# Small experts and extra slots as whole float32 matmuls on column tiles of the array, with unsplit weights

## Chip, cores and metric

The kernel runs on one core of a Trainium2 chip. Its time is the device time of one execution in microseconds. The engines are named as in the profile: PE (TensorE matmul), PEld (its weight loads), DVE (VectorE), ACT (ScalarE), POOL (GpSimd) and SP (SyncE, which here issues the weight transfers).

## What is computed

The reference is two layers of a decoder trunk over 256 tokens of width 1024. In each layer three token mixers (S5, SSD, gated DeltaNet) are followed by a feed-forward part: a dense SwiGLU in the first layer, and in the second eight SwiGLU experts of which each token uses two. The change lies in the second layer's experts alone:

```python
def moe_ffn(h, w_router, w_gate, w_up, w_down):
    logits = (h @ w_router).astype(jnp.float32)
    top_v, top_i = lax.top_k(logits, TOP_K)
    ...
    for e in range(N_EXPERTS):
        out = out + combine[..., e:e + 1].astype(h.dtype) * swiglu(h, w_gate[e], w_up[e], w_down[e])
    return out
```

`swiglu(h)` is `(silu(h @ w_gate) * (h @ w_up)) @ w_down`, with gate and up of 1024 x 3584 and down of 3584 x 1024, all float32. Eight experts have 352 MB of weights, which pass through the chip once.

## The kernel before

**Slots.** An expert works only on the tokens that chose it. `route` ranks the tokens of each expert, and a one-hot matrix gathers them into slots (`take_in`, tile `xe`) and later puts the results back (`put_back`). Experts 0, 1 and 7 have 128 slots ("wide"), the others 64 ("small"), and expert 7 has 16 more ("few", the extra slots). If an expert has more tokens than its slots, a general path (`general`, `expert`) runs in place of `stream`; the inputs here take `stream`.

**Precision.** Every weight is split into a high part in float32r (`his`, a copy on ACT) and a low part (`los`, a subtraction on DVE); `stage` does that for a load of 128 x 2048 values. A wide product is three float32r matmuls, in `mm3`: high by high, high by low, low by high. A small expert has its 64 tokens' high and low parts side by side in 128 columns of the array, so two matmuls (with `his` and with `los`) make all four products (`half_up`, `half_down`). Its accumulator has 128 rows then, high and low, and they are summed as they are transposed, by a matmul with a matrix of ones (`turn_sum`, tile `pmts`). The extra slots are done alike, in 32 columns (`pmf`, `pfd`), with their down products added up in the SBUF (`accf`).

**Steps.** An expert's 3584 hidden columns are done in 7 steps of 512. A step has the gate and up products (`pmg`), the gate (`sg`, or `gf` and `sgs`), its transposition (`pmt` of a wide expert, `pmts` of a small one), and the down products (`macc`), which come one step later. It uses 6 loads of 1 MiB: two of gate, two of up, two of down. `STEPS` orders the steps: expert 2 alone, expert 0 alone, then seven rounds of one step of expert 7 with three steps of experts 3, 4 and 5, then expert 1 alone and expert 6 alone. The gather of a coming expert is cut into pieces that stand between a step's products (`GATHER`, `gap`).

**Transfers.** The loads go through a ring of ten slots of 1 MiB (`ringb` 0 to 4, then `ringa` 0 to 4), all issued by SP in the order of use. A load waits until what last read its slot is done: in before that is `stage`. Before the routing four loads are staged ahead (two with GpSimd as the subtracting engine, into `extra`), and the first step's gate and up products stand ahead of the branch between `stream` and `general`.

**Order.** A scheduler orders the instructions of each engine when the program is built, with its own estimate of times; engines then run their queues in order.

Of the kernel before, what the change touches and what calls it, by code (L numbers as in the profile page):

```python
# [27 lines left out]
# schedule: engines of the first layer's S5 weights, offsets of priority of the mixers' parts (by layer), pieces of the last  # L28
# weights, engines of the first staged weights, the order around the FFN, and the steps of it beside the second S5 weights
# [5 lines left out]
TP = [2, 2, 4, 2, 0, 1]  # L35
MO = [[0, 1, 1, 1], 1]
# [9 lines left out]
def tile_hymba_trunk(ctx: ExitStack, tc: tile.TileContext, p: dict, out: bass.AP):  # L46
# [43 lines left out]
    # ------------------------------------------------------------------ constants  # L90
# [67 lines left out]
    # columns: norm_mix 0, norm_ffn 16, ssd conv 32, its bias 88, ssd_norm 102, s5_norm 108, gdn_norm 112  # L158
# [21 lines left out]
    # ------------------------------------------------------------------ helpers  # L180
# [23 lines left out]
    def stage(src, after=None, parts=1, on=V):  # L204
        k, n = src.shape[1], src.shape[2]
        pool, words = cur['stg']
        if isinstance(pool, list):
            his, los = pool
            h, l = (q[cur['sn'] % len(q)][:, :k * n].rearrange("p (k n) -> p k n", k=k) for q in (his, los))
            cur['sn'] += 1  # L210
            for o in pieces(k, n, parts):
                if after is None:
                    A.activation(out=h[o], in_=src[o], func=AF.Copy)  # L213
                else:
                    A.activation(out=h[o], in_=src[o], func=AF.Identity, scale=after)
                on.tensor_tensor(out=l[o], in0=src[o], in1=h[o].bitcast(F32), op=OP.subtract)  # L216
            return h, l
        h = pool.tile([128, words], F32R, name="whi", tag="whi")[:, :k * n].rearrange("p (k n) -> p k n", k=k)
        l = pool.tile([128, words], F32R, name="wlo", tag="wlo")[:, :k * n].rearrange("p (k n) -> p k n", k=k)
        cur['last', 'A'] = A.activation(out=h, in_=src, func=AF.Copy)  # L220
        cur['last', 'V'] = on.tensor_tensor(out=l, in0=src, in1=h.bitcast(F32), op=OP.subtract)  # L221
        return h, l
# [18 lines left out]
    def exact_exp(o, x, t, q):  # L241
        """o = exp(x) to float32 accuracy; t, q: scratch like x."""
# [24 lines left out]
    def rows_rstd(pool=None):  # L267
        """of X: the rows' mean squares (with the norm's guard) and their reciprocal roots"""
# [10 lines left out]
    def along(r, pool):  # L279
        """a column [128, 2] of the tokens as a row in each partition"""  # L280
# [7 lines left out]
    def rows_T(wcol, pool, scaled=False):  # L288
        """X, scaled by the norm's weight, transposed and split; the rows' scale is put on after the products"""
# [22 lines left out]
    # ------------------------------------------------------------------ S5 weights  # L312
# [8 lines left out]
    # powers of the discretised poles, for both layers: [state, layer * tile]  # L321
# [8 lines left out]
    def s5_small():  # L330
# [55 lines left out]
        # unit phases exp(i theta 2^k), k = 2..7, brought back to modulus 1 on the way  # L386
# [24 lines left out]
    def s5_prep(l, keep, ET, EB, EC, tag="S"):  # L411
        """in three steps"""
# [11 lines left out]
        # rotation tables over 64 positions, step exp(4 i theta)  # L424
# [12 lines left out]
        # input matrices [state, tile, 4 positions of a block, 32 channels]  # L437
# [28 lines left out]
        # output matrices  # L466
# [25 lines left out]
        # lag matrices, with the skip weight on the diagonal  # L492
# [21 lines left out]
    # ------------------------------------------------------------------ mixers  # L514
# [63 lines left out]
    def layer_mix(l, pm):  # L578
# [26 lines left out]
        # ---- GDN projections  # L605
# [11 lines left out]
        # gates  # L617
# [3 lines left out]
        for n in range(2):  # L621
# [6 lines left out]
            # without the rows' scale  # L628
# [14 lines left out]
        # softplus = max(x,0) + log1p(exp(-|x|)), log1p(e) = 2 atanh(e/(2+e))  # L643
# [37 lines left out]
        # sums of squares of q, k per token and head  # L681
# [23 lines left out]
        # (in the second layer the S5 scratch lies beside its weights, and is free with them before the rest is)  # L705
# [3 lines left out]
        with scope("late", "right"):  # L709
# [21 lines left out]
            # ---- GDN token-layout operands  # L731
# [24 lines left out]
            # ---- GDN pair matrices  # L756
# [66 lines left out]
            # ---- GDN recurrence over the two chunks  # L823
# [17 lines left out]
            def gdn_out(n):  # L841
                # norm per head, gate
# [7 lines left out]
                # of 64 times the mean; the eight that its root lacks is in the norm's weight  # L850
# [51 lines left out]
            # ---- S5  # L902
# [10 lines left out]
            with using(pm):  # L913
                mark('ssdp', l)
                # ---- SSD
# [56 lines left out]
                    # states shifted by one position, rotated back  # L972
# [19 lines left out]
                    # 2*gelu  # L992
                    # beyond |y| = 12 the tanh is 1 in float32
# [29 lines left out]
                    # squares of 2^-10 y, limited so that their sum stays finite; a mean square that  # L1023
                    # float32 cannot hold has a zero reciprocal root
# [29 lines left out]
            with scope("ssd"):  # L1054
# [62 lines left out]
                # the gates are without the rows' scale: the guard is over its square  # L1117
# [26 lines left out]
        # ---- output projection  # L1144
# [84 lines left out]
    # ------------------------------------------------------------------ MoE  # L1229
    def route(split_rows, cw, rk, cnt, one, r):  # L1230
        caps = act.tile([1, 8], F32, name="caps")
        G.memset(caps, 64.0)
        for e in range(NE):
            if SLOTS[e] != 64:
                G.memset(caps[:, e:e + 1], SLOTS[e] + 16.0 * (e == MANY))
# [18 lines left out]
        with ExitStack() as st:  # L1254
            if MO[1]:
# [4 lines left out]
        # the two largest, the first of equal ones first  # L1260
# [13 lines left out]
        # exclusive count of equal ones before, plus the number above  # L1274
# [3 lines left out]
        # (of these the inclusive count is at most two)  # L1278
# [3 lines left out]
        # rank of a token among the tokens of an expert, from one on; zero where it isn't one  # L1282
# [6 lines left out]
        def rest():  # L1289
# [7 lines left out]
            V.tensor_scalar(out=one, in0=rk[:, 0, 0:1], scalar1=0.0, scalar2=1.0, op0=OP.mult, op1=OP.add)  # L1297
            # the weights of the two, with the rows' scale of what the experts return
# [4 lines left out]
            # (the table of the gates is loaded here)  # L1303
# [9 lines left out]
    # the stream of experts: their slots, those interleaved, those gathered together, and the one with sixteen slots more  # L1313
    SLOTS = {0: 128, 1: 128, 2: 64, 3: 64, 4: 64, 5: 64, 6: 64, 7: 128}
    # (of the expert with more, a step to each three of the small ones beside it)
# [7 lines left out]
    PLACE = {(2, 0): (256, 64), (0, 0): (0, 128), (7, 0): (256, 128), (7, 128): (512, 16), (3, 0): (0, 64), (4, 0): (128, 64),  # L1323
# [502 lines left out]
```

## Time and profile before

| | |
|---|---|
| median of 3 runs | 1725.63 us (1724.66 to 1727.02) |
| profiled execution, span | 1727.2 us |
| busy PE, DVE, ACT | 95%, 79%, 61% |
| transfers over the span | 435.89 MB, mean 252 GB/s |

The profiled execution's own time is its span, from the first to the last instruction. Busy time of PE runs high, because matmuls are pipelined and each is shown with its modelled end; the distance from start to start tells what one costs.

### The profile page before, as it was taken

The numbers are of one execution on the slowest core, as the hardware profiler recorded it, in microseconds if no ns is written. First come the engines' busy times: TensorE is split into PE (matmuls) and PEld (weight loads), VectorE is DVE, ScalarE is ACT, GpSimd is POOL, SyncE is SP. The second block draws the span as 40 slices with busy tenths as digits, with TensorE's granted clock in tenths as the row PEclk, the third lists the DMA queues.
The fourth block names the chain that finished last, engine by engine and source line by source line (L and its number), as shares of the span: only waits on it lengthen the run. The fifth ranks groups of instructions, "written<-read, shape, count | busy, mean of one in ns | idle before, by whom it ended". The sixth has DMA issues, their size and how long they took to land.

```text
span 1727.2 us, 24692 instructions
## 1 busy us (share of the span) xinstructions
PE 1632.8 (95%) x9535; PEld 1369.3 (79%) x9535; DVE 1360.3 (79%) x1684; ACT 1061.4 (61%) x1202; POOL 231.9 (13%) x286
## 2 busy tenths in 40 slices
PE   5889979999999998899999999999999999999996
PEld 5889869999989896777887777777777777788774
DVE  7886765545579876699987788797878979988997
ACT  5543354443364434588776577676767777777885
POOL 6910270100001003240010002000211001000000
PEclk9999989999999898799999999999999999999999
DMA  6421045555554234499999698998989999999993
GB/s 180 141 68 50 21 143 195 171 184 183 166 153 125 96 123 172 166 388 393 392 362 333 233 363 316 344 360 307 353 307 354 334 348 314 365 340 366 366 392 128
DMA packets 214798, 435.89 MB, mean 252 GB/s; under 512 B 11083, under 2 KB 64420, under 8 KB 214672
## 3 DMA queue, kind: packets, MB, share of 16 engines
q1 hardware_dynamic: 211824, 431.66, 70.7%
q0 software_dynamic: 928, 1.43, 0.4%
q8 instruction: 77, 1.26, 0.3%
q10 hardware_dynamic: 1920, 1.13, 0.2%
q14 instruction: 49, 0.40, 0.1%
HBM read 433.15 MB, written 1.05 MB: 251 GB/s over the span
## 4 chain that ended last, share of the span: by engine, by line
PE 78%; DVE 10%; ACT 4%; DMA 3%; POOL 3%; issue 2%; DVEq 0%; SPq 0%; ACTq 0%; POOLq 0%
PE pmg L1431 11%; PE macc L1552 7%; PE pmg L227 5%; PE pmg L228 5%; PE pmg L226 5%; DVE los L216 4%; PE pmts L1530 4%; PE pmf L1431 3%; PE macc L227 2%; PE macc L228 2%; PE macc L226 2%; ACT his L213 2%; DMA raw<-in_w_in_dram 2%; PE acc L226 2%; PE acc L227 2%
## 5 line engine op out<-in xcount | busy, mean ns | idle before, releaser
L216 DVE TENSOR_TENSOR los<-ringa,his 128x2048 fp32r<-128x2048 f32 (+2 forms) x171 | 377.3, 2226 | 56.5 <-PE pmf L1431 17.4
L216 DVE TENSOR_TENSOR los<-ringb,his 128x2048 fp32r<-128x2048 f32 (+1 forms) x172 | 380.4, 2226 | 49.0 <-PE pmf L1431 11.2
L213 ACT ACTIVATE his<-ringb 128x2048 fp32r<-128x2048 f32 (+1 forms) x174 | 322.8, 1864 | 87.6 <-PE pmg L228 22.1
L213 ACT ACTIVATE his<-ringa 128x2048 fp32r<-128x2048 f32 (+1 forms) x167 | 314.5, 1894 | 90.2 <-PE pmg L228 21.2
L220 ACT ACTIVATE whi<-raw 128x1024 fp32r<-128x1024 f32 (+3 forms) x110 | 148.1, 1355 | 189.6 <-issue 80.9
L221 DVE TENSOR_TENSOR wlo<-raw,whi 128x1024 fp32r<-128x1024 f32 (+3 forms) x109 | 179.5, 1649 | 102.0 <-ACT whi L220 101.7
L1431 PE MATMUL pmg<-los,xe 128*128 128x512 f32 x552 | 156.3, 406 | 10.9 <-DVE los L216 10.6
L1431 PE MATMUL pmg<-his,xe 128*128 128x512 f32 x556 | 155.2, 406 | 1.5 <-ACT his L213 1.5
L1431 PEld LDWEIGHTS pmg<-los,xe 128*128 128x128 f32 x552 | 101.3, 191 | 42.3 <-DVE los L216 21.3
L227 PE MATMUL pmg<-los,xe 128*128 128x512 f32 x336 | 133.0, 396 | 0.8 <-DVE los L216 0.8
L228 PE MATMUL pmg<-his,xe 128*128 128x512 f32 x336 | 132.4, 394 | 0.0
L226 PE MATMUL pmg<-his,xe 128*128 128x512 f32 x336 | 132.2, 399 | 0.0
L1431 PEld LDWEIGHTS pmg<-his,xe 128*128 128x128 f32 x556 | 104.8, 193 | 27.2 <-ACT his L213 3.6
L1552 PE MATMUL macc<-los,hs 128*128 128x512 f32 x280 | 82.8, 412 | 1.8 <-DVE los L216 1.5
L1375 POOL TENSOR_SCALAR oh<-iota_f,rkk 128x256 fp32r<-128x256 f32 (+1 forms) x16 | 31.3, 1968 | 380.4 <-PE pxe L1381 380.4
L1552 PE MATMUL macc<-his,hs 128*128 128x512 f32 x280 | 80.0, 399 | 1.5 <-ACT his L213 1.3
L227 PEld LDWEIGHTS pmg<-los,xe 128*128 128x128 f32 x336 | 63.3, 188 | 17.7 <-DVE los L216 3.2
L226 PEld LDWEIGHTS pmg<-his,xe 128*128 128x128 f32 x336 | 63.2, 188 | 16.3 <-ACT his L213 1.1
L228 PEld LDWEIGHTS pmg<-his,xe 128*128 128x128 f32 x336 | 63.1, 188 | 14.1
L226 PE MATMUL pfg<-hT_hi,whi 128*128 128x256 f32 x224 | 63.6, 284 | 9.4 <-DVE xr_t L236 9.4
L227 PE MATMUL macc<-los,ht 128*128 128x512 f32 x168 | 66.2, 394 | 2.6 <-DVE los L216 2.5
L1375 POOL TENSOR_SCALAR od<-iota_f,rkk 128x128 fp32r<-128x128 f32 x18 | 38.1, 2127 | 220.7 <-PE ptoh L1392 220.7
(650 smaller groups left out, 3668.9 us busy)
## 6 DMA issues: line engine op xcount, KB each, us to landing
ringb<-in_moe_w_gate_dram SPq DMA_DIRECT2D x57, 1024.0 KB, 6.7
ringb<-in_moe_w_up_dram SPq DMA_DIRECT2D x55, 1024.0 KB, 6.7
ringa<-in_moe_w_up_dram SPq DMA_DIRECT2D x55, 1024.0 KB, 7.2
ringa<-in_moe_w_down_dram SPq DMA_DIRECT2D x55, 1024.0 KB, 7.0
ringa<-in_moe_w_gate_dram SPq DMA_DIRECT2D x53, 1024.0 KB, 6.1
ringb<-in_moe_w_down_dram SPq DMA_DIRECT2D x53, 1024.0 KB, 6.3
raw<-in_w_in_dram SPq DMA_DIRECT2D x16, 1024.0 KB, 5.9
raw<-in_ff_w_gate_dram SPq DMA_DIRECT2D x14, 1024.0 KB, 5.1
```

The source lines that it names most:

```text
L213: A.activation(out=h[o], in_=src[o], func=AF.Copy)
L216: on.tensor_tensor(out=l[o], in0=src[o], in1=h[o].bitcast(F32), op=OP.subtract)
L220: cur['last', 'A'] = A.activation(out=h, in_=src, func=AF.Copy)
L221: cur['last', 'V'] = on.tensor_tensor(out=l, in0=src, in1=h.bitcast(F32), op=OP.subtract)
L226: T.matmul(o, lhsT=lh, rhs=rh, start=start, stop=False)
L227: T.matmul(o, lhsT=lh, rhs=rl, start=False, stop=False)
L228: T.matmul(o, lhsT=ll, rhs=rh, start=False, stop=stop)
L1375: on.tensor_scalar(out=dst[:, i].rearrange("p (r n) -> p r n", n=n), in0=io, scalar1=rk[:, i, e:e + 1], scalar2=-float(first), op0=OP.subt ...
L1431: T.matmul(pp, lhsT=x[:, kh * 4 + kk, :], rhs=w[:, kk, :], start=kh + i + kk == 0, stop=kh + i + kk == 5)
L1530: T.matmul(pt[:, q, c, :], lhsT=x, rhs=sm[q][:2 * n], start=i == 0, stop=i == len(gs) - 1)
L1552: T.matmul(acc[f], lhsT=h[:, c2 * 2 + cc].rearrange("p h s -> p (h s)"), rhs=w3[i][:, cc, f * 512:f * 512 + 512], start=ends[0] and i + cc ...
```

## The change

Small experts no longer split anything. Their tokens' rows are kept as float32 (`xs`), and the weights are read as they land in the ring, by float32 matmuls with 64 columns. Two such matmuls go to the two halves of the array: the gate product to columns 0 to 63, the up product to columns 64 to 127, and in the down products the two halves of the output columns. The extra slots are 32 now, and go to four tiles of 32 columns, two of them for each of gate and up (the contraction's even and odd blocks), summed as they are transposed. Gate and up of a small step end up in one accumulator, and one transposition of four 128 x 128 blocks gives both. For this a load now holds 256 rows of gate and the same 256 rows of up, in two transfers of 512 KiB (`load_up`). Wide experts keep `mm3`, on loads in the new form.

The staging ahead of the routing, the first step ahead of the branch and the small pieces of the last weights go. What else the diff has is comments taken out.

```diff
+        def load_up(e, m, k2):
+            slot = cur['ring'][cur['pos'] % len(cur['ring'])]
+            cur['pos'] += 1
+            v = slot[:, :2048].rearrange("p (k n) -> p k n", k=4)
+            for q, w in enumerate((wg, wu)):
+                nc.sync.dma_start(v[:, 2 * q:2 * q + 2], w[e][256 * k2:256 * k2 + 256, m * 512:m * 512 + 512]
+                                  .rearrange("(k p) n -> p k n", p=128))
+            return v
...
-        def half_up(pp, x, w3, kh):
-            for i, w in enumerate(w3):
-                for kk in range(4):
-                    T.matmul(pp, lhsT=x[:, kh * 4 + kk, :], rhs=w[:, kk, :], start=kh + i + kk == 0, stop=kh + i + kk == 5)
+            def half_up(pp, x, w, k2):
+                for kk in range(2):
+                    k = 2 * k2 + kk
+                    for q in range(2):
+                        T.matmul(pp[64 * q:64 * q + 64], lhsT=x[:, k, :], rhs=w[:, 2 * q + kk, :], start=k == 0, stop=k == 7,
+                                 tile_position=(0, 64 * q), skip_group_check=True)
+            def few_up(pp, x, w, k2):
+                for j in range(4):
+                    T.matmul(pp[32 * j:32 * j + 32], lhsT=x[:, 2 * k2 + j % 2, :], rhs=w[:, j, :], start=k2 == 0, stop=k2 == 3,
+                             tile_position=(0, 32 * j), skip_group_check=True)
...
+            def half_down(acc, h, w, c2, m):
+                for cc in range(2):
+                    c = c2 * 2 + cc
+                    for f in range(2):
+                        T.matmul(acc[64 * f:64 * f + 64], lhsT=h[:, c, :], rhs=w[:, cc, f * 512:f * 512 + 512],
+                                 start=m == 0 and c == 0, stop=m == 6 and c == 3, tile_position=(0, 64 * f), skip_group_check=True)
...
-        # the first step's weights are staged before the rows are there
-            ready = [f() for f in first[:len(cur['ring'])]]
-                    ready[i] = stage(ready[i], on=(V, G)[MO[0][i]])
-            ready += [f() for f in first[len(ready):len(ready) + 4]]
+            ready = [f() for f in w_loads(STEPS[0][0])[:len(cur['ring'])]]
...
+                    for k2 in range(4):
+                        w = take(ups[e])
+                        if wide:
+                            wide_up(pgu, rows(e), stage(w), k2)
+                        else:
+                            half_up(pgu[0], rows(e), w, k2)
                         if many:
-                            pgf.append(ps("G", "pmf")[:32])
+                            few_up(pgf, rows(e, 128), w, k2)
...
+                        g = act.tile([128, 512], F32, name="gs", tag="gs")
+                        A.activation(out=g, in_=pgu[0], func=AF.Identity, scale=rs)
```

On PE, in the middle of expert 2, a step of before reads (`los` and `his` are the split weights, `gf` the gate and up rows):

```order
L1431 MATMUL pmg<-los,xe 128x512 x8
L1431 MATMUL pmg<-his,xe 128x512 x4
L1552 MATMUL macc_25546<-his,hs 128x512
L1552 MATMUL macc_25547<-his,hs 128x512
L1552 MATMUL macc_25546<-his,hs 128x512
L1552 MATMUL macc_25547<-his,hs 128x512
L1530 MATMUL pmts<-sr,gf 128x64 x4
L1431 MATMUL pmg<-los,xe 128x512 x4
```

and of the changed kernel, from one step's transposition to the next, with pieces of the gather (`pxe`) between:

```order
L1511 MATMUL pmts<-ident,gs 128x128 x4
L1476 MATMUL pmg<-ringb_7016,xs 64x512 x4
L1476 MATMUL pmg<-ringb_7017,xs 64x512 x4
L1476 MATMUL pmg<-ringb_7018,xs 64x512 x4
L1476 MATMUL pmg<-ringb_7019,xs 64x512 x4
L1379 MATMUL pxe<-oh,hn_h 128x256 x2
L1379 MATMUL pxe<-oh,hn_l 128x256 x2
L1534 MATMUL macc<-ringb_7020,hs 64x512 x4
L1379 MATMUL pxe<-oh,hn_h 128x256 x2
L1379 MATMUL pxe<-oh,hn_l 128x256 x2
L1534 MATMUL macc<-ringa_7021,hs 64x512 x4
```

The 48 matmuls of a small step on split weights have become 24 on column tiles, four to a load, straight from the ring.

In the rounds, the extra slots' matmuls (`pmf`) stand between wide ones (`his`, `los`) of the same load, on PE in the changed kernel:

```order
L219 MATMUL pmg<-his,xe 128x512 x2
L1482 MATMUL pmf<-ringa_7022,xs 32x512
L220 MATMUL pmg<-los,xe 128x512
L221 MATMUL pmg<-his,xe 128x512
L219 MATMUL pmg<-his,xe 128x512
L220 MATMUL pmg<-los,xe 128x512
```

Here one of four `pmf` is apart from the other three, which come after eight more wide matmuls; most stand four together.

On ACT, where a round begins, the changed kernel has (`hs` is a small step's silu, `gs` its gate and up rows, `his` the copies of expert 7's weights, `sg` that expert's gate):

```order
L1684 ACTIVATE gs<-pmg,rsl 128x512
L1550 ACTIVATE y<-macc 128x512
L1504 ACTIVATE hs<-pmts 128x256
L213 ACTIVATE his<-ringb_7018 128x2048
L213 ACTIVATE his<-ringb_7019 128x2048
L213 ACTIVATE his<-ringb_7020 128x2048
L213 ACTIVATE his<-ringa_7021 128x2048
L1687 ACTIVATE gf<-pmf 128x512
L1487 ACTIVATE sg<-pmg,rsl 128x512
```

In before a copy `his` stood between almost any two other instructions of ACT; now the four of a wide step's gate and up stand together, behind the silu of the small step ahead of them.

## Rows read from the trace of the kernel before

**Rows 1.** The page: busy time by engine.

```profile
PE 1632.8 (95%) x9535; PEld 1369.3 (79%) x9535; DVE 1360.3 (79%) x1684; ACT 1061.4 (61%) x1202; POOL 231.9 (13%) x286
```

**Rows 2.** Stretches (busy PE, PEld, DVE, ACT, POOL; clock, DMA share, GB/s): expert 2, rounds.

```profile
740.00:840.00 100.00, 95.44 (x455) 75.71 (x454) 96.16 (x62) 83.14 (x70) 18.48 (x6) 1.00 1.04 392
963.30:1489.50 526.20, 514.06 (x2453) 393.14 (x2452) 439.19 (x316) 377.97 (x338) 46.04 (x21) 0.99 0.92 332
```

**Rows 3.** Timeline of PE: starts of transposes that end wide steps.

```profile
824.93 0.60 PE L1509 MATMUL pmt<-ident,sg 128*128 128x128 f32 x4
...
963.31 0.60 PE L1509 MATMUL pmt<-ident,sg 128*128 128x128 f32 x4
...
1489.46 0.38 PE L1509 MATMUL pmt<-ident,sg 128*128 128x128 f32 x2
...
1564.57 0.27 PE L1509 MATMUL pmt<-ident,sg 128*128 128x128 f32 x1
...
1581.62 0.27 PE L1509 MATMUL pmt<-ident,sg 128*128 128x128 f32 x1
...
1598.67 0.27 PE L1509 MATMUL pmt<-ident,sg 128*128 128x128 f32 x1
```

**Rows 4.** Chain of waits, 1400 to 1480: start, time, engine, line, count.

```profile
1400.37 1.85 PE pmf L1431 x8
...
1431.95 0.47 PE pxe L1381 x4
...
1454.02 2.80 PE macc L1552 x12
...
1457.29 1.73 PE pmts L1530 x16
```

**Rows 5.** Groups of instructions from 740 us to the end, VectorE and ScalarE.

```profile
L216 DVE TENSOR_TENSOR los<-ringb,his 128x2048 fp32r<-128x2048 f32 (+1 forms) x168 | 371.2, 2225 | 45.3 <-PE pmf L1431 11.2 <-PE pmg L1431 6.7 <-PE pmg L227 6.0
L213 ACT ACTIVATE his<-ringa 128x2048 fp32r<-128x2048 f32 (+1 forms) x162 | 305.0, 1893 | 83.3 <-PE pmg L228 21.2 <-PE macc L228 16.7 <-PE pmg L1431 12.7
L1532 ACT ACTIVATE sgs<-pmts 128x256 f32<-128x256 f32 (+1 forms) x40 | 13.9, 347 | 17.8 <-PE pmts L1530 17.8
```

**Rows 6.** Line 1706, whole float32 of 512 columns: durations, then timeline.

```profile
L1706 PE MATMUL psc<-X,ident x8: 590/592/648, 1698.6 to 1709.1; 128*128 128x512 f32 x8
...
1708.67 1.02 PE L1706 MATMUL psc<-X,ident 128*128 128x512 f32 x2
```

**Rows 7.** Column tiles in the mixers: line 503, then timelines.

```profile
L503 PE MATMUL ptlag<-cm,wb x112: 196/244/298, 101.9 to 104.9; 128*32 128x128 f32 x28, 128*32 128x96 f32 x28, 128*32 128x64 f32 x28, 128*32 128x32 f32 x28
...
108.04 2.44 PE L949 MATMUL puv<-UC,ident 128*32 128x128 f32 x32 [1.00 <-DVE lag L511]
...
193.01 0.61 PE L833 MATMUL pw<-vb,DT 128*128 128x64 f32 x4
193.55 0.45 PE L870 MATMUL pS<-vnew,kend 128*64 128x64 f32 x6
```

**Rows 8.** Timeline of SP: the 17th transfer of the experts' weights.

```profile
724.81 0.38 SPq L197 DMA_DIRECT2D ringa<-in_moe_w_gate_dram  x1
```

**Rows 9.** The routing: a scan's durations, and timelines of POOL and PE.

```profile
L1276 DVE TENSOR_TENSOR_SCAN cu<-eq,ng x2: 216/2000/3785, 690.0 to 693.7; 128x8 f32<-128x8 f32 x2
...
688.26 5.47 POOL L216 TENSOR_TENSOR extra<-ringb,extra 128x2048 fp32r<-128x2048 f32 x1
...
702.04 1.09 PE L1431 MATMUL pmg<-his,xe 128*128 128x512 f32 x4
```

**Rows 10.** Stretches with the granted clock, columns as in rows 2.

```profile
101.00:105.00 4.00, 4.00 (x122) 3.75 (x120) 3.55 (x14) 3.00 (x8) 0.00 (x0) 1.00 0.08 13
712.00:723.00 11.00, 10.69 (x42) 9.83 (x43) 2.47 (x5) 4.62 (x4) 3.86 (x5) 0.54 0.28 99
965.50:972.30 6.80, 6.80 (x23) 5.83 (x23) 1.88 (x6) 2.39 (x3) 1.23 (x2) 0.50 0.38 150
```

**Rows 11.** Line 1660, the last products: durations, first and last start.

```profile
L1660 PE MATMUL psc<-y,ohT x8: 389/395/507, 1713.9 to 1715.9; 128*128 128x512 f32 x8
```

More of the change, by code (lines that the diff above doesn't have):

```diff
@@ L210, in stage @@
             cur['sn'] += 1
[L211 to L221, printed above, removed]
+        else:
+            h, l = (pool.tile([128, words], F32R, name=t, tag=t)[:, :k * n].rearrange("p (k n) -> p k n", k=k)
+                    for t in ("whi", "wlo"))
+        A.activation(out=h, in_=src, func=AF.Copy)
+        on.tensor_tensor(out=l, in0=src, in1=h.bitcast(F32), op=OP.subtract)
         return h, l
@@ L1630, in down @@
                     if m == 0:
-                        acc[e] = [ps("P" if wide else "S", f"macc{f}") for f in range(2)]
+                        if wide:
+                            acc[e] = [ps("P", f"macc{f}") for f in range(2)]
+                        else:
+                            acc[e] = ps("S", "macc")
                         if hf is not None:
-                            acc['few'] = act.tile([32, 2, 512], F32, name="accf")
+                            acc['few'] = ps("S", "maccf")
@@ L1634, in down @@
                     for c2 in range(2):
-                        n = parts(e, m, 1 + c2)
-                        last = e == steps[-1][0] and m == 6 and c2 and TP[5]
-                        if last:
-                            V.tensor_scalar(out=one.bitcast(I32), in0=(ht[:, 0, 0:1] if wide else ht[:, 0, 0, 0:1]).bitcast(I32), scalar1=0,
-                                            scalar2=0x3f800000, op0=OP.bitwise_and, op1=OP.bitwise_or)
-                        w3 = staged(take(downs[e]), n, one if last else None, G if e == steps[-1][0] and m == 5 and TP[4] >> c2 & 1 else V)
@@ L1661, in down @@
                         final(lambda n, f: pzs[n, f], cur['wF'])
                     elif m == 6:
-                        few = [([acc['few'][:, f] for f in range(2)], ots[e, 128])] if hf is not None else []
-                        late.extend(put_back(e, (acc[e], ots[e, 0]), *few))
+                        few = [(acc['few'], ots[e, 128])] if hf is not None else []
+                        if wide:
+                            late.extend(put_back(e, (acc[e], ots[e, 0]), few))
+                        else:
+                            late.extend(put_back(e, None, [(acc[e], ots[e, 0])]))
@@ L1688, in stream @@
-                    if m == 0:
-                        sums[e] = None if wide else scaled(sum64, e)
-                        if many:
-                            sums['few'] = scaled(sum16, e, 128)
-                    g = gate(pgu, rsl[:, RS[e, 0]:RS[e, 0] + 1]) if wide else keep(pgu, "gs") if i else None
-                    gf = keep(pgf, "gf") if many else None
+                    pgu = [ps("G", "pmg") for q in range(1 + wide)]
+                    pgf = ps("G", "pmf") if many else None
@@ new lines, in stream @@
+                    for k2 in range(4):
+                        w = take(ups[e])
+                        if wide:
+                            wide_up(pgu, rows(e), stage(w), k2)
+                        else:
+                            half_up(pgu[0], rows(e), w, k2)
+                        if many:
+                            few_up(pgf, rows(e, 128), w, k2)
+                        if late and k2 % 2:
+                            late.pop(0)()
+                    if m == 0 and many:
+                        sm['few'] = act.tile([128, 2, FEW], F32, name="sr")
+                        G.tensor_scalar(out=sm['few'], in0=sums, scalar1=rsl[:, RS[e, 128]:RS[e, 128] + 1], scalar2=None, op0=OP.mult)
@@ L1694, in stream @@
+                    rs = rsl[:, RS[e, 0]:RS[e, 0] + 1]
+                    if wide:
+                        g = gate(pgu, rs)
+                    else:
+                        g = act.tile([128, 512], F32, name="gs", tag="gs")
+                        A.activation(out=g, in_=pgu[0], func=AF.Identity, scale=rs)
+                    if many:
+                        gf = act.tile([128, 512], F32, name="gf")
+                        A.activation(out=gf, in_=pgf, func=AF.Copy)
                     gap()
```

250 lines of the change are left out of this document (100 added, 150 removed).

## The prediction

> **What bounds the kernel now.** I read the page first, then the stretches of the second layer's experts, then single instructions. The page gives PE 95%, VectorE 79% and ScalarE 61% of the span [rows 1], an average over stages with different limits. So the second layer's experts, which take the last 1000 us, have to be taken apart. The stretches do that [rows 2]. The experts run in five stages: expert 2 (64 slots) alone, expert 0 (128 slots) alone, seven rounds in which one step of expert 7 stands beside three steps of experts 3, 4 and 5, expert 1 alone, expert 6 alone. While a small expert is alone the DMA engines are full (392 GB/s, share 1.04). In the rounds they are not (332 GB/s, share 0.92) although PE is busy for 514 of 526 us: there PE is the bound, and VectorE follows with 439 us.
>
> The starts of the transposes that end a wide step date the stages [rows 3]. Two of them lie 17.05 us apart (1564.57 to 1581.62), which is a wide step without anything beside it. From 963.31 to 1489.46 go seven rounds: 75.2 us each. The chain of waits prices PE's work when it runs without gaps [rows 4]: a float32r matmul of 512 columns costs 0.233 us (2.80 for 12), one of the extra slots 0.231 (1.85 for 8), a summing transpose 0.108 (1.73 for 16), a gather's matmul 0.118 (0.47 for 4); a plain transpose is taken like a summing one, 0.11. A small step has 48 such matmuls and 16 summing transposes, so 11.2 + 1.7 = 12.9 us; expert 7's extra slots add 48 x 0.231 + 16 x 0.108 = 12.8 us. A round is then 17.05 + 12.8 + 3 x 12.9 + about 3 for gathers and put-backs = 71.5 us; the 3.7 us to 75.2 are waits.
>
> The splits of the weights, the other half of a small step, are subtractions of 2.2 us on VectorE (168 on one half of the ring alone) and copies of 1.9 us on ScalarE [rows 5]. A small step has 6, so 13.4 us of VectorE. That is hidden behind 6 loads, each 1,048,576 bytes / 392 GB/s = 2.675 us, together 16.05 us, when the expert is alone.
>
> **What the change costs on PE.** No row of before has a whole-float32 matmul on weights in the ring, so its price comes from others. A float32 matmul of 512 columns stands in the trace as two passes: line 1706 issues four, the records are eight [rows 6]. Two of them take 1.02 us with the last one's 0.59 in it, so their starts lie 0.43 us apart; 28 passes of 128 columns on line 503 fill 3.05 us [rows 7], 0.85 ns a column, or 0.436 for 512. I take 0.43: one matmul is 0.86 us, against 0.466 for the two split ones that it replaces. So the change pays only if column tiles run beside each other. They do in before: line 503 issues four column tiles of 128, 96, 64 and 32 columns, 28 passes each, started between 101.9 and 104.9; one after the other, at 0.43 / 512 us a column, they would need 7.5 us, and the longest tile alone needs 3.0, which is what they took. Line 870 alternates two tiles of 64 rows in the order of the new code. I take two tiles at the price of one, 0.86 us a pair, and four at the same. The other end is line 949, where 32 passes over four tiles took 2.44 - 0.27 + 0.11 = 2.28 us instead of 0.86: an overlap of 1.5 only. Its code gives each tile eight passes in a row before the next tile, and the new code two, so line 503 (four in a row) is the nearer row.
>
> A small step is 12 pairs: 8 for gate and up, 4 for down. The scheduler cuts some groups of four apart (in the order shown, a single one stands between wide matmuls); counted over the whole order, 441 pairs and 56 fours are left instead of 420 and 42. So a small step costs 12.6 x 0.86 + 4 x 0.11 = 11.3 us (before 12.9), the extra slots 8 x 0.86 + 0.9 = 7.8 us (before 12.8). The order has 304 changes between whole array and tiles. Line 833's four matmuls before line 870 are 0.112 us apart (0.61 less an end of 0.275, by three), so the next was due at 193.46 and started at 193.55, 0.09 us late [rows 7]; at 0.095 a change that is 29 us, some 3.2 in a round. The Trainium skill (TensorEngine Tiling, Key Properties) says that changing the tiling mode drains the engine; this trace agrees, with that 0.09 us.
>
> A round of PE work is then 17.05 + 7.8 + 33.8 + 3 + 3.2 = 64.8 us. The loads of a round need 24 x 2.675 = 64.2. Both being so near, waits no longer hide: in the order shown ScalarE has the four copies of expert 7's weights right behind the last small gate, so PE stands for a silu (0.35) and one copy (1.9) [rows 5] before the wide matmuls, some 2.3 us, and about 1 us for gates. I take 68 us (64.2 and 75 are the ends). Before, such waits were 3.7 us.
>
> **What it does to the start.** Before, four loads are split ahead of the routing; this frees four ring slots, so fourteen loads are under way early; but the 17th leaves only at 724.81 [rows 8], behind the splits that follow. The change takes the early splits out: only ten loads are there when the experts begin. On the other hand the routing is shortened. Of two scans of VectorE that are alike one took 0.22 us and one 3.79, beside a subtraction of 5.47 us on GpSimd, which goes; and a copy of 1.9 us [rows 5] ahead of the routing goes on ScalarE. Without them the first products, at 702.04 before [rows 9], could begin 5 us earlier, but they now stand behind the branch: I take 700, and 705 for the first new load, which on the 17th's place is 705 + 6 x 2.675 = 721 (the clock was at 0.54 from 712 to 723, after a pause there [rows 10], and may fall again).
>
> **The sum, by the dates of rows 3.** The wide expert 0 needs loads 43 to 46 first: 705 + 36 x 2.675 + 7 for a split and its products = 808 for its first transposes (824.93 before, so -17). To expert 7's first, at 963.31: six or seven wide steps, gathers of 32 x 0.118 twice, put-back, four fours: 134 us where 138.4 stood (-4). Rounds 7 x 68 = 476 against 526 (-50). Expert 1 is wide and PE-bound, 109.2 us as before (0). At its end the ring of ten is full, since PE lagged; 34 loads remain, 91 us, more than the 84 of PE. Behind the last load stand two pairs, one split, eight products and the final norm, from the last product at 1715.9 to the end 11.3 us [rows 11]; with 1.7 for the pairs, 1.9 for the products and some 2 for the split that is 17 us. That is 108 against 1727.2 - 1598.67 = 128.5 (-20.5). In all -92: a span of 1635. The runs' median, 1725.6, lies 1.6 under the profiled span, so 1634.
>
> SP issues ten transfers in a step instead of six; at 0.38 us each [rows 8] that is 3.8 of 16 us, hidden behind the transfers themselves.
>
> **The rivals.** (1) *Transfers bind throughout*: PE's waits fit in the slack. 326 loads from 705 on are 872 us, and 17: 1594. Rows 2 speak for it (small experts alone do run at 392), the PE sum of 64.8 in a round against it. (2) *The tiles overlap 1.5-fold*, as in line 949: a pair costs 1.14, a round 45.8 x 0.28 = 13 us more, expert 6 becomes PE-bound (110 us for 91): 1635 + 90 + 19 = 1744, slower than before. It decides from a pair of about 1.11 us on. Against it stand lines 503 and 870. The Trainium skill (TensorE: Matmul & The Clock Gate, Measured speedup vs the span model) gives 2.38-fold for three column tiles; taken as two at 1.59, a pair would be an estimated 1.08 us and the end near 1719, no change to speak of; this trace does not agree, since line 503 reaches 7.5 / 3.05 = 2.5-fold, all that its longest tile allows. (3) *The clock falls to half in the small steps*: tiles leave PE waiting for loads a third of the time. Then a pair is 1.72, a round 107, the end about 2040; from a quarter of that time at half clock on, it is slower. For it: the clock was 0.50 from 965.5 to 972.3, behind the transposes of 963.31 and narrow summing ones [rows 3, 10]. Against it: 1.00 from 101 to 105, where nearly all is column tiles of 32. (4) *Halved loads are slower*, say 350 GB/s: 326 x 3.0 + 17 + 705 = 1700. Nothing shows it but the smaller pieces at the end.
>
> **The numbers.** The forecast 0.66, rival 1 0.13, 2 0.08, 3 0.05, 4 0.08. The range goes from rival 1 to just past rival 4: 1594 to 1712. A measurement of this kernel tells 0.2% from nothing. Rivals 2 and 3 with a few of the rest are slower (0.12), a narrow strip between 2 and 4 is the same (0.03), the others faster (0.85).
>
> **What would show it.** Starts of one tile's passes on lines 1476 and 1534 at 0.43 us with the other tile's beside them show the pair's price; 0.57 or more is rival 2. Transposes of expert 7 some 68 us apart (64 is rival 1, over 78 a miss), the first wide transposes near 808, 392 GB/s for experts 2 and 6, a granted clock of 1.00 through the rounds, and 17 us behind the last load show the rest. I am wrong if PE waits long inside a block of tiles for something no row here shows.

## The result and the profile after

The changed kernel takes 1682.68 us (median of 4 runs, 1677.65 to 1687.83) where the kernel before took 1725.14 in the same comparison (4 runs, 1723.61 to 1727.02): a ratio of 0.9751, 95% interval 0.9729 to 0.9773, or 42.5 us less. The forecast was 1634, 91 us less. The sign and the range (1594 to 1712) hold; 42.5 of the 91 us came. The profiled execution has a span of 1679.3 us.

The page, busy time by engine, to set beside [rows 1]:

```profile
PE 1574.3 (94%) x9043; PEld 1077.4 (64%) x9043; DVE 851.3 (51%) x1341; ACT 643.1 (38%) x890; POOL 164.5 (10%) x273
```

VectorE and ScalarE have lost the splits of the small experts (1360 and 1061 us before). PE's share has hardly moved, so what the change did to the time has to be read by stage. The timeline of PE of the changed kernel, the transposes that end wide steps, for [rows 3]:

```profile
804.79 0.66 PE L1494 MATMUL pmt<-ident,sg 128*128 128x128 f32 x4
...
943.77 0.60 PE L1494 MATMUL pmt<-ident,sg 128*128 128x128 f32 x4
...
1446.54 0.66 PE L1494 MATMUL pmt<-ident,sg 128*128 128x128 f32 x4
...
1556.49 0.60 PE L1494 MATMUL pmt<-ident,sg 128*128 128x128 f32 x4
```

Four dates divide the time into five stages, in us:

| | before | forecast | after | after less forecast |
|---|---|---|---|---|
| to expert 0's first transposes | 824.9 | 808 | 804.8 | -3.2 |
| expert 0, to expert 7's first | 138.4 | 134 | 139.0 | +5.0 |
| seven rounds | 526.2 | 476 | 502.8 | +26.8 |
| expert 1 | 109.2 | 109.2 | 110.0 | +0.8 |
| its last transposes to the end | 128.5 | 108 | 122.8 | +14.8 |
| span | 1727.2 | 1635 | 1679.3 | +44 |

The stretches of the changed kernel (columns as in [rows 2]): expert 2, the rounds, the end in three parts, and a stretch just behind a round's start:

```profile
740.00:780.00 40.00, 37.77 (x166) 12.61 (x165) 1.61 (x4) 4.05 (x9) 4.19 (x6) 1.00 1.04 395
943.77:1446.54 502.77, 481.78 (x2145) 211.32 (x2143) 132.58 (x115) 127.62 (x150) 16.16 (x18) 0.98 0.95 349
1062.90:1066.40 3.50, 3.50 (x16) 1.41 (x9) 3.02 (x2) 2.09 (x2) 0.00 (x0) 0.51 1.04 383
1556.49:1597.00 40.51, 38.59 (x149) 16.21 (x149) 11.17 (x12) 7.42 (x9) 0.00 (x0) 0.96 0.95 336
1597.00:1659.00 62.00, 57.62 (x260) 20.20 (x258) 1.68 (x4) 5.52 (x11) 0.00 (x0) 1.00 1.03 393
1659.00:1679.30 20.30, 7.16 (x32) 2.05 (x28) 5.84 (x18) 3.49 (x10) 0.00 (x0) 0.78 0.13 54
```

Loads of two pieces run at 395 GB/s while expert 2 is alone, as before. In the rounds they run at 349, with PE busy for 482 of 503 us, so PE seems to set the rounds still; the run half_products below tests that. The price of a product is right, as the timeline of PE in expert 2 shows:

```profile
729.72 7.09 PE L1476 MATMUL pmg<-ringa,xs 128*64 128x512 f32 x32
736.74 0.50 PE L1379 MATMUL pxe<-oh,hn_h 128*128 128x256 f32 x2
```

The 32 passes are eight pairs of matmuls. The gather behind them starts 7.02 us after the first of them: 16 x 0.43, and 0.14 for the change between tiles and whole array. Two tiles cost what one costs. The extra time stands where a round begins. On PE:

```profile
1054.93 0.66 PE L1511 MATMUL pmts<-ident,gs 128*128 128x128 f32 x4 [0.87 <-ACT gs L1684]
1055.51 3.65 PE L1534 MATMUL macc<-ringa,hs 128*64 128x512 f32 x16
1061.45 0.73 PE L219 MATMUL pmg<-his,xe 128*128 128x512 f32 x2 [2.28 <-ACT his L213]
1062.11 1.20 PE L1482 MATMUL pmf<-ringb,xs 128*32 128x512 f32 x8
```

and at the same place on ScalarE:

```profile
1054.19 0.69 ACT L1684 ACTIVATE gs<-pmg,rsl 128x512 f32<-128x512 f32 x1 [6.57 <-PE pmg L1476]
1059.21 0.38 ACT L1504 ACTIVATE hs<-pmts 128x256 f32<-128x256 f32 x1 [4.34 <-PE macc L1534]
1059.49 5.50 ACT L213 ACTIVATE his<-ringb 128x2048 fp32r<-128x2048 f32 x3
```

Three things are to be seen. PE stands for `gs` before the transposes (0.87), and again for the first copy `his` (2.28). ScalarE itself stands idle for 4.34 us ahead of the silu, and what ends that is not the transposes, which were done by 1055.6, but PE's down products `macc`: they are the last readers of the one buffer that `hs` has, and the copies queue behind. And from 1062.90 the granted clock is 0.51, the lower of its two levels (1.2 GHz of 2.4).

To see what each of these costs, I went through all starts of PE in the rounds and charged each distance to the next start: first its price (a pass on tiles 0.4295, a float32r product 0.2335, a gather 0.118, a transpose 0.109), the rest to a change between whole array and tiles (the instructions on both sides of it), to a stretch at half clock, or, over 0.25 us, to a wait. In us, with the number of changes in brackets; the other rows are the experiments below:

| rounds of | at price | changes | half clock | waits | other | sum |
|---|---|---|---|---|---|---|
| changed kernel | 434.1 | 33.7 (208) | 9.7 | 23.2 | 2.0 | 502.8 |
| two_hs | 434.1 | 34.4 (215) | 1.7 | 11.2 | 2.5 | 483.7 |
| fours_together | 419.5 | 22.5 (142) | 12.3 | 28.7 | 3.8 | 486.7 |
| turn_between | 435.8 | 36.6 (231) | 7.9 | 11.9 | 1.5 | 493.7 |
| two_hs_fours | 419.5 | 22.6 (144) | 4.4 | 19.0 | 4.7 | 470.2 |
| two_hs_fours_turn | 419.5 | 22.7 (145) | 2.9 | 17.6 | 4.5 | 467.2 |
| staged_ahead | 428.1 | 30.5 (204) | 4.4 | 13.3 | 2.9 | 479.2 |
| half_products | 324.6 | 27.7 (166) | 16.1 | 68.0 | 1.3 | 437.6 |

### The profile page after: what moved, and what is told of

It reads as the page before. It is cut to its first block, busy times and chain, and to the rows that moved or that the text cites. A ratio compares the mean times of both kernels' runs of the same rounds, so it can differ in the third digit from the quotient of the medians.

```text
span 1679.3 us, 22923 instructions
## 1 busy us (share of the span) xinstructions
PE 1574.3 (94%) x9043; PEld 1077.4 (64%) x9043; DVE 851.3 (51%) x1341; ACT 643.1 (38%) x890; POOL 164.5 (10%) x273
## 3 DMA queue, kind: packets, MB, share of 16 engines
HBM read 433.15 MB, written 1.05 MB: 259 GB/s over the span
## 5 line engine op out<-in xcount | busy, mean ns | idle before, releaser
L214 DVE TENSOR_TENSOR los<-ringa,his 128x2048 fp32r<-128x2048 f32 x64 | 146.3, 2290 | 78.2 <-ACT his L213 45.1
L214 DVE TENSOR_TENSOR los<-ringb,his 128x2048 fp32r<-128x2048 f32 x62 | 141.7, 2291 | 60.4 <-PE pmg L220 33.0
L1476 PE MATMUL pmg<-ringb,xs 128*64 128x512 f32 x584 | 146.1, 604 | 3.5 <-issue 3.4
L220 PE MATMUL pmg<-los,xe 128*128 128x512 f32 x336 | 139.9, 416 | 3.6 <-DVE los L214 3.6
L219 PE MATMUL pmg<-his,xe 128*128 128x512 f32 x336 | 124.9, 411 | 17.8 <-ACT his L213 17.0
L213 ACT ACTIVATE his<-ringa 128x2048 fp32r<-128x2048 f32 x64 | 121.4, 1911 | 41.8 <-PE pmg L221 26.9
L221 PE MATMUL pmg<-his,xe 128*128 128x512 f32 x336 | 135.5, 403 | 0.0
L1476 PE MATMUL pmg<-ringa,xs 128*64 128x512 f32 x536 | 135.1, 598 | 0.3 <-DMA ringa<-in_moe_w_up_dram 0.3
L213 ACT ACTIVATE his<-ringb 128x2048 fp32r<-128x2048 f32 x62 | 117.8, 1913 | 42.4 <-PE pmg L221 29.3
L220 PEld LDWEIGHTS pmg<-los,xe 128*128 128x128 f32 x336 | 64.8, 193 | 42.4 <-issue 18.1
L219 PEld LDWEIGHTS pmg<-his,xe 128*128 128x128 f32 x336 | 63.1, 194 | 42.6 <-ACT his L213 23.2
L221 PEld LDWEIGHTS pmg<-his,xe 128*128 128x128 f32 x336 | 65.0, 194 | 13.6
L219 PE MATMUL pfg<-hT_hi,whi 128*128 128x256 f32 x224 | 63.3, 283 | 9.4 <-DVE xr_t L229 9.4
```

The source lines that it names most:

```text
L219: T.matmul(o, lhsT=lh, rhs=rh, start=start, stop=False)
L220: T.matmul(o, lhsT=lh, rhs=rl, start=False, stop=False)
L221: T.matmul(o, lhsT=ll, rhs=rh, start=False, stop=stop)
L1476: T.matmul(pp[64 * q:64 * q + 64], lhsT=x[:, k, :], rhs=w[:, 2 * q + kk, :], start=k == 0, stop=k == 7, tile_position=(0, 64 * q), skip_gr ...
```

## The experiments

All times are medians of 4 runs (10 for the last), and ratios are to the kernel before, measured beside them; a ratio differs from the quotient of the medians by up to 0.002. The comparison with the changed kernel goes by the ratios, 0.001 being 1.7 us. The diffs are cut to the lines that matter.

**A second buffer for hs.**

```diff
-                h = act.tile([128, 4, n], F32, name="hs", tag=tag)
+                h = act.tile([128, 4, n], F32, name="hs", tag=tag, bufs=2)
```

> A small step's gate rows (hs) get a second buffer; the queues of PE, SP and GpSimd stay as they are but for two or three rows. Theory A (PE's waits and PE's work set the rounds): the silu no longer waits for the down products of the step before, so the copies behind it on ScalarE start some 3 us earlier and PE's 2.45 us of waiting ahead of each of seven wide steps falls to 0.3 or less, 15 us; and if the clock falls to half only because of that wait, the 9.7 us that it costs in the rounds and 1.7 at expert 6's start go as well: 26 us in all, about 1657, ratio 0.985. Theory B (the clock falls for what the column tiles do, not for the wait): the wait goes and the half clock stays, 15 us, 1668. Theory C (the transfers set the rounds): under 5 us, the wait moves to a load.

Measured: 1668.99 us, ratio 0.9652 (0.9622 to 0.9682), 17 us faster than the changed kernel. In the profiled execution the rounds are 19.1 us shorter. ScalarE at the start of the same round:

```profile
1062.33 0.69 ACT L1684 ACTIVATE gs<-pmg,rsl 128x512 f32<-128x512 f32 x1 [8.45 <-PE pmg L1476]
1063.76 0.38 ACT L1504 ACTIVATE hs<-pmts 128x256 f32<-128x256 f32 x1 [0.75 <-PE pmts L1511]
1064.04 5.50 ACT L213 ACTIVATE his<-ringb 128x2048 fp32r<-128x2048 f32 x3
```

The silu now follows its transposes, the copies 1.7 us behind `gs` instead of 5.3, and PE's wide products find them. The groups of PE from 700 us on give what is left of the wait in all, changed kernel first (busy, mean ns, idle before and its releasers):

```profile
L219 PE MATMUL pmg<-his,xe 128*128 128x512 f32 x336 | 124.9, 411 | 17.8 <-ACT his L213 17.0 <-ACT xs L1420 0.8
```

and with two buffers:

```profile
L219 PE MATMUL pmg<-his,xe 128*128 128x512 f32 x336 | 123.8, 408 | 6.5 <-ACT his L213 5.7 <-ACT xs L1420 0.8
```

The half clock nearly goes with it, from five stretches and 9.7 us of loss in the rounds to one and 1.7; that one follows the one wait of 2.7 us that is left (1269.5 us). The stretch of the rounds, to set beside that of the changed kernel:

```profile
951.91:1435.63 483.72, 474.05 (x2145) 208.15 (x2143) 132.81 (x115) 128.04 (x150) 16.22 (x18) 1.00 0.97 361
```

The time alone, 17 us, would lie nearer B's 15 than A's 26; what speaks for A is the clock in the trace. The work on the tiles is the same, most of the waits are gone, and the falls went with them: here they come behind the waits and not from the tiles. A had the size too large by the waits at two wide steps' starts that stayed, 2.7 us at 1269.5 and 2.3 from 1417 on. Not every such wait is followed by a fall: in the changed kernel the one of 2.5 us at 1133.0 is not. Nor does every fall follow a wait. In the kernel before, the clock fell at 1269.3 though PE had been busy throughout, the last of it with 21 transposes from 1265.34 on and, from 1267.87, products of 512 columns:

```profile
1262.00:1269.30 7.30, 7.30 (x43) 5.86 (x42) 6.00 (x5) 5.56 (x8) 3.59 (x2) 1.00 0.65 221
1269.30:1272.70 3.40, 3.40 (x10) 2.62 (x9) 2.17 (x1) 1.86 (x2) 0.01 (x1) 0.50 1.03 386
```

**The extra slots' products together.**

```diff
                         if many:
-                            few_up(pgf, rows(e, 128), w, k2)
+                            fw.append(w)
+                            if k2 % 2:
+                                with tc.issue_after(last_wide[0].ins):
+                                    for j in (k2 - 1, k2):
+                                        few_up(pgf, rows(e, 128), fw[j], j)
```

`few_down` likewise; `last_wide` is the last product of `mm3`.

> The extra slots' products of two loads stand together, eight column tiles in a block behind the wide products. In the order, changes between whole array and tiles go from 298 to 222, blocks of four cut apart go (56 fours become 42). Theory A (PE's work sets the rounds and a change costs the 0.163 us that the trace after shows): 76 x 0.163 + 14 x 0.86 = 24 us, 1658, ratio 0.986. By the 0.095 us of the forecast: 19 us, 1663. Theory C (transfers set the rounds, or a load's slot held longer by the block costs as much): under 5 us.

Measured: 1671.39 us, ratio 0.9677 (0.9659 to 0.9694), 13 us faster. The table shows the expected parts, 14.6 us of products and 11.2 of changes (66 of them, 0.17 each), and what a third of it turned into: 5.5 us of waits and 2.6 of half clock. At a wide step's start PE stands for the copies as before, and then a second time, for their low parts:

```profile
1062.07 1.94 PE L1536 MATMUL macc<-ringa,hs 128*64 128x512 f32 x8
1066.29 0.74 PE L221 MATMUL pmg<-his,xe 128*128 128x512 f32 x2 [2.28 <-ACT his L213]
1068.61 0.80 PE L222 MATMUL pmg<-los,xe 128*128 128x512 f32 x1 [1.59 <-DVE los L214]
```

In the changed kernel blocks of fours stood there (`pmf` at 1062.11) and covered the second wait.

**Transposes between the halves of the down products.**

```diff
+                    if prev and not wide and SLOTS[prev[0]] == 64:
+                        with tc.issue_after(half_way[0].ins):
+                            h = turn_half(g)
```

`half_way` is the last matmul of the first half; elsewhere `turn` or `turn_half` stands as before.

> A small step's transposes are pinned behind the first half of the down products of the step before, so that PE has four passes to do while ScalarE writes gs. Theory A: the waits of 1.0 us on gs at six places in the rounds and six at the end go, 12 us; the order has 16 more changes of the array, 2.6 us: 9 us faster, 1673, ratio 0.994. Theory C, or if the gap only moves: 0 to 3 us, and up to 3 us slower from the changes.

Measured: 1675.39 us, ratio 0.9688 (0.966 to 0.9715), 11 us faster, close to what A gave. The waits of the transposes on `gs` fell from 12.9 to 1.7 us, by the group of that line, changed kernel first:

```profile
L1511 PE MATMUL pmts<-ident,gs 128*128 128x128 f32 x140 | 22.7, 283 | 12.9 <-ACT gs L1684 12.9
L1511 PE MATMUL pmts<-ident,gs 128*128 128x128 f32 x140 | 22.5, 283 | 1.7 <-ACT gs L1688 1.7
```

The end kept its length (122.5 us), though A had counted six of its waits; the rounds are 9.1 us shorter.

**Half of the small products left out.**

```diff
-                for kk in range(2):
+                for kk in range(1):
                     k = 2 * k2 + kk
```

and the same for `cc` in `half_down`.

> Every small expert leaves out half of its gate, up and down products (one of two blocks of each load); all transfers stay. It asks for the floor by transfers. Theory A (PE's work sets the rounds): the seven rounds fall to the 64.2 us of their loads, at most 66, 43 to 53 us less, and expert 6 to 91 + 17 us, 14 less: 1615 to 1628, ratio 0.96 to 0.968. Theory C (transfers set the rounds already, at less than 392 GB/s): within 10 us of the changed kernel. A mixed case, some 1640, would say that waits which no work covers are left.

Measured: 1614.55 us, ratio 0.9346 (0.9326 to 0.9366), 70 us faster. The rounds fell to 62.5 us, with transfers at 390 GB/s. Stretches: rounds, then the end's middle part.

```profile
948.22:1385.82 437.60, 377.89 (x1640) 174.44 (x1638) 132.38 (x114) 129.16 (x150) 16.16 (x18) 0.96 1.03 390
...
1535.00:1598.00 63.00, 45.34 (x130) 12.49 (x126) 1.84 (x5) 5.22 (x11) 0.00 (x0) 0.81 1.00 380
```

That is near the transfers' floor: the last four rounds take 63.3 to 64.0 us, where the forecast had 64.2 for their 24 loads. So PE's work is what holds the changed kernel's rounds, 71.8 us each, some 8 or 9 us above it. At the end it is the other way round: though 35 us of passes are gone there, the time from expert 1's last transposes to the end is 119.4 us, against 122.8. The transfers set the end, but for these 3 us.

**Both and all three edits.**

> Both edits together: the second buffer of hs, and the extra slots' products of two loads in one block. Run alone they gave 17 and 13 us against the changed kernel. In the rounds the edit of the fours alone took 14.6 us of products and 11 us of changes away and lost 8 us of that to waits ahead of the wide steps and to the half clock behind them, which the second buffer takes away. Theory A: with both, the rounds fall to 63.7 us of work each and little waiting, 65 to 67 us, 455 to 470 in all, and the time to 1645 to 1655, ratio 0.956. Theory C (near the 64.2 us of loads the waits move to the loads): the two gains do not add, 1658 or more.

Measured: 1649.97 us, ratio 0.9564 (0.9539 to 0.9589), 32 us faster than the changed kernel; the two gains alone were 17 and 13. They add.

> The two edits and the transposes of small steps between the halves of the down products, here with no more changes of the array than without (222). Theory A: the waits of 1.0 us on gs in the rounds go too, some 6 us: 1638 to 1650, ratio 0.953. Expert 6 at the end, on transfers at 395 GB/s from some 1600 on, gains nothing. Theory C: no faster than with two edits.

Measured: 1648.67 us, ratio 0.9536 (0.9515 to 0.9558), the fastest of these kernels that do all the work, though not told apart from the run before it; the profiled rounds are 3.0 us shorter, half of what A gave. In its rounds the transfers reach 374 GB/s and PE still stands for 17.6 us, most of it at wide steps' starts: 0.57 for a copy and 1.76 for a low part, five times.

**The next wide step's loads split ahead.** On top of the three edits:

```diff
+                    if not wide and i + 1 < len(steps) and SLOTS[steps[i + 1][0]] == 128 and prev:
+                        for _ in range(2):
+                            w = take(ups[steps[i + 1][0]])
+                            early.append((w, stage(w)))
```

> To the three edits comes a fourth: the first two loads of a wide step that follows a small one are taken and split ahead of the small step's last down products, so that the copies stand between gs and hs on ScalarE. The order has 270 changes of the array instead of 222. Theory A: of the 17.6 us of waits and 2.9 us of half clock left in the rounds some 13 go (the 2.3 us at a wide step's start, six times); the 48 changes cost 8: 3 to 6 us faster than with three edits, rounds of 66 us, 1643 to 1646. If a change costs the 0.095 us of the forecast: 8 to 10 us faster. Theory C (the loads set the rounds by now, 64.2 us each): the waits move to loads, 0 to 5 us slower.

> As the run before, but the two loads are split ahead of the small step's gs: the order on PE is the same, ScalarE has the copies before gs. Theory A: where loads are ahead, ScalarE does the copies in its idle time and the result is that of the run before, within 3 us. Theory C: the copies wait for their loads and gs behind them, PE stands for gs: up to 2 us in each of eight places, 10 to 16 us slower than the run before.

Measured: 1664.23 us (0.9654, 0.9623 to 0.9686) and 1661.15 us (0.9639, 0.9605 to 0.9672), by the ratios 20 and 18 us slower than without, by the medians 16 and 12. In the profiles the rounds are 12.0 and 13.2 us longer. This was a miss: neither theory gave so much. The order pulled the wide products forward by as much as the copies, so that a wait at the wide step's start stayed, 2.2 us of idle time here:

```profile
1059.72 0.66 PE L1513 MATMUL pmts<-ident,gs 128*128 128x128 f32 x4
1060.75 0.50 PE L221 MATMUL pmg<-his,xe 128*128 128x512 f32 x1 [0.37 <-ACT his L213]
1063.08 0.52 PE L222 MATMUL pmg<-los,xe 128*128 128x512 f32 x1 [1.83 <-DVE los L214]
```

Small blocks were cut apart instead: 59 more changes (7.8 us) and 20 more passes (8.6 us) in the rounds. That the two runs agree within 3 us shows that copies ahead of `gs` did not hold it up.

**Eight passes in a row on each tile.**

```diff
-                for kk in range(2):
-                    k = 2 * k2 + kk
-                    for q in range(2):
+                for q in range(2):
+                    for kk in range(4):
+                        k = 2 * k2 + kk
```

with two loads taken together.

> Gate and up products of two loads together, and of these all four blocks of the gate (eight passes on one tile) ahead of the four of up, where the changed kernel alternates the tiles matmul by matmul. The order has fewer changes of the array too (248 for 298, 8 us). Reading D, from the line of four tiles with eight passes each that overlapped 1.5-fold only: such a block of sixteen passes takes 16 x 0.43 / 1.5 = 4.6 us and not 3.44; 2.3 us more in each of 35 small steps, those of expert 2 and 6 partly hidden by loads: 50 to 70 us slower than the changed kernel, 1730 to 1750. Reading E (a tile's passes do not hold back those of the other, whatever the order): passes of both tiles start together, 3.44 us, and some 8 to 15 us faster from the fewer changes.

Measured: 1728.44 us, ratio 1.0017 (0.9995 to 1.0039): the whole gain of the change is gone. The same 32 passes of a step, in expert 2:

```profile
738.75 8.97 PE L1476 MATMUL pmg<-ringa,xs 128*64 128x512 f32 x32
747.65 0.50 PE L1379 MATMUL pxe<-oh,hn_h 128*128 128x256 f32 x2
```

8.90 us to the next start where the alternating order takes 7.02: 32 x 0.43 / 8.90 is an overlap of 1.55, that of line 949 in [rows 7]. Reading D holds. The 46 us are less than D's 50 to 70. In the profile 25.5 of them are in the rounds and 10.9 in expert 2 (122.7 us for 111.8 from its first product to the first wide transposes); the end, where expert 6 has slack behind its loads, is 0.7 longer. Why the rounds lost no more was not taken apart.

## Why the prediction came out as it did

**The price of a pair** (0.86 us) was right: passes 0.43 apart, two tiles together. So was the choice of line 503 over line 949 by the number of passes in a row. Rival 2 falls for the order as it is written, and eight_in_a_row shows that it would have come true with another order of the same matmuls. The products of a round came to 434.1 / 7 = 62.0 us, where the forecast had 61.6 (64.8 less 3.2 for changes).

**The price of a change** was too low, and this is the first step that failed. The forecast read 0.09 us from one switch into tiles and took 0.095. The changed kernel gives 33.7 / 208 = 0.16 on the mean, and the 66 changes that fours_together takes away gave back 0.17 each: 4.8 us a round and not 3.2, 11 us in all. Line 833 into line 870 [rows 7] shows one direction, and only the first instruction behind the change. The timeline of PE inside a round shows the rest:

```profile
1069.07 0.73 PE L219 MATMUL pmg<-his,xe 128*128 128x512 f32 x2
1069.73 1.05 PE L1482 MATMUL pmf<-ringb,xs 128*32 128x512 f32 x4
1070.71 0.50 PE L220 MATMUL pmg<-los,xe 128*128 128x512 f32 x1
1071.05 0.40 PE L221 MATMUL pmg<-his,xe 128*128 128x512 f32 x1
1071.29 0.40 PE L219 MATMUL pmg<-his,xe 128*128 128x512 f32 x1
```

Two wide products, 0.47 us by price, take 0.66 up to the tiles; two passes on tiles, 0.86, take 0.98; the first wide product behind takes 0.34 and only the next 0.24. The second instruction behind a change is late too, by 0.1 us on the whole array. The same lateness stands behind a pause without a change: at 828.32, after 0.8 us of idle time, the first wide product takes 0.33 to the next.

**The waits of a round** were right in size and place, 23.2 / 7 = 3.3 us for the forecast's 3.2: one copy and one silu where a wide step begins. The size is in part luck, since their cause was only half seen. The forecast had the copies behind the silu, and did not ask what the silu waits for: the one buffer of `hs`, which the down products of the step before release. That made the copies late although ScalarE was idle. Without that wait, in two_hs, the same order of copies behind the silu leaves 11.2 us of waits in seven rounds, and the second buffer, a change of one word, brings 17 us.

**The clock** was the second step that failed. Rival 3 had the clock fall in the small steps, and the forecast set it aside because it stayed at 1.00 in a stretch full of tiles. It does stay there (1.00 in expert 2). It falls to half where a wide step begins behind a wait of some 2.5 us, five times in the rounds: 9.7 us lost, where before lost 4.7 by the same count. Outside the rounds it did so at 786.4, where expert 0 begins, and at 1571.5, where expert 6 begins. In the kernel before, the 3.7 us a round that the forecast read as waits held some 0.7 of the clock's loss already; the waits among them were 2.1. The forecast had such a fall before it, at 965.5 [rows 10]; the same trace has PE idle for 1.0 us ahead of 964.92. Having written down the pauses of the changed kernel, it could have charged them with the clock as well.

**The end** was the third, 14.8 us of the miss. The forecast counted 34 loads left at full rate, 91 us, and 17 behind the last. By the stretches above, 40.51 x 336 + 62 x 393 are 38.0 MB from expert 1's last transposes on, some 36 loads of 1.05 MB without the final norm's weight: two loads more (5 us). For the first 40 us they came at 336 GB/s (6 us), as their slots were not yet free: in that stretch SP waits 32.7 us in all, 22.9 of it for PE's products of expert 6's first steps and 4.9 for the last splits of expert 1. And 20.3 us and not 17 followed the last load. That transfers bind there, as the forecast had it, half_products shows.

**Expert 0** took 139.0 us for the 134: 4 us of split products went as forecast (127.0 to 119.6, with 3.4 for passes), and a wait of 1.0 at 827.3, changes of 1.0, and 2.5 us spread over some 510 wide products, 5 ns each, took them back. **The start** came at 804.8, with 808 forecast, and that is luck in part. The profiled execution has expert 2's first products at 693.0, where the forecast had 700, and then 111.8 us to the transposes, where it had 108. Of the other kernels with the same order up to their first products, two have these at 692.3 and 694.3 and five at 700.1 to 700.7, with the wide transposes at 811.9 to 813.2.

With these steps mended (products 62.0, changes 4.8, waits 3.3, half clock 1.4, other 0.3) a round is 71.8. Of the miss of 44 us, 27 lie in the rounds (11 changes, 10 half clock, 3 products, 3 the rest), 15 at the end and 5 in expert 0; the start gave 3 back. Rivals 1 and 4 fall: transfers bind at the end and in expert 2 alone, and they run at 393 to 395 GB/s there.

## What to carry to other kernels

Two column tiles shared the array's time in full when they alternated matmul by matmul, and 1.55-fold with eight passes in a row on each: write the tile loop innermost. Keep blocks on tiles together, since each change between tiles and whole array cost about 0.16 us here and shows on the second instruction behind it as well. When a change makes two resources nearly equal, price the waits at each stage's start by following the releaser of the in-order queue's first waiting instruction to its buffer, and add what the clock loses behind such pauses of PE. Of a stage that two engines share, ask with a run that leaves work out which of them sets it, stage by stage: here PE in the rounds, the transfers at the end.

## What the runs showed of the hardware

Tiles overlap as far as the order lets them. The Trainium skill (TensorEngine Tiling (Array Packing), Key Properties) says that different tiles can load weights and multiply in parallel; the trace agrees where the two tiles alternate (7.02 us for 32 passes), and with eight passes in a row on each the same tiles overlap 1.55-fold only (8.90 us).

In these rounds the granted clock fell to half mostly where a wide step began behind pauses of PE, idle for 2.3 to 2.8 us in the changed kernel, and in two_hs_fours_turn behind 0.4 and 1.6 us in turn (two falls for five such places). With the pauses gone the falls were gone, and with more pauses (half_products, 68 us of waits) the loss at half clock rose to 16.1 us. One fall of the kernel before, at 1269.3, has no pause ahead of it, so pauses are not all of it; what else makes it fall is not shown.

The stretch ahead of the experts differs between executions: expert 2's first transposes stand at 702.0 to 704.1 us in three of these profiles and at 710.6 to 711.4 in five others, of kernels whose order up to there is the same. Where the difference arises was not followed up; it is a reason to compare stages and not only spans.
